# Three pieces of another size, two groups of loads put behind the token tiles, and a sum of squares spread later, in a one-core decoder layer

## The chip, the cores and the metric

The kernel runs on one core of one Trainium2 chip. Its metric is the device time of one execution in microseconds; of several executions the median counts. The core has five engines that work side by side: PE (TensorE, matrix products; its weight loads are listed as PEld), DVE (VectorE), ACT (ScalarE), POOL (GpSimd) and SP (SyncE, which here only issues DMA transfers). Each engine executes its own list of instructions in order; where an instruction needs a result of another engine or of a transfer, it waits, and all that stands behind it on that engine waits too.

## The reference

One decoder layer is applied to 1024 prompt tokens and to 64 sample tokens (8 sequences of 8) that have a cached past. All is in float32, with 1024 features.

```python
h = rmsnorm(x, lw['g_mix'])
proj = h @ lw['w_in']                       # columns: RWKV | short convolution | stick-breaking attention
o_rw, wkv_new, shift_new = rwkv7_mixer(p_rw, shift_prev, wkv_prev, lw)
o_cv, conv_new = short_conv_mixer(cb, cc, cx, conv_prev, lw['conv_w'])
o_sb = stick_breaking(q, k_all, v_all, past_len, lw['sb_bias'])
x = x + concatenate([o_rw, o_cv, o_sb]) @ lw['w_out']
h2 = rmsnorm(x, lw['g_mlp'])
x = x + square(relu(h2 @ lw['w_up'])) @ lw['w_down']
gate = sigmoid(rmsnorm(x, lw['g_ple']) @ lw['w_ple_gate'])
x = x + gate * (p @ lw['w_ple_proj'])
```

Here `rmsnorm(x, g)` is `x * rsqrt(mean(x * x) + 1e-6) * g`. In `rwkv7_mixer` each of 4 heads carries a 64x64 state through the tokens. Outputs are x, the new keys and values, and the new states.

## The kernel before

A float32 product is made of three: operand and weight are each split into a rounded high part and the rest (`wh` and `wl`, `h_hi` and `h_lo`, by a cast on ACT and a subtraction on POOL or DVE), and `wh*hi`, `wh*lo` and `wl*hi` are added up in one of eight banks of PSUM (b0 to b7), 512 columns each. Features lie on the partitions, tokens along the free axis. All 1088 tokens are worked on at once up to the mixers' outputs; from the output projection on they are two groups, A (tokens 0 to 511) and B (512 to 1087, in two pieces of 288 columns).

The stages, in the time of the profile:

- **Front, 0 to 39 us.** Nine tiles of 128 tokens (the ninth: the 64 samples) are loaded (L110), squared and summed on ACT (L189, L190), scaled on DVE (L193), transposed on PE (L198), and cast and split (L200 on ACT, L201 on DVE). SP's list holds further loads: the first weights of `w_in` (L156), 11 short loads of parameter rows into `prow` (L213, transposed at L218), 5 of small weights (L300 to L302) and the shift state `sh` (L308). The buffer `xt` has four copies: the load of tile 4 can start once tile 0 has been read.
- **RWKV projections, to 174 us.** `rw_tile` works through the tokens in the three pieces of `CH`; each is 24 products (L169 to L171) into one of banks 0 to 2. The pieces of `CH` are also used by the low-rank products, the norm of the keys, the bonus (L446 on PE, with the matrix `bones`; L447 on DVE) and the convolution.
- **Query, key and value projections, 150 to 240 us.** Groups of products (L795 to L797) fill banks 0 and 1 in turn. A bank is read by ACT twice (L802 copy `nat`, L805 square `sq`); DVE sums and scales (L807, L809, L810); PE transposes `nat` (L844). In the same stretch DVE works the function `wkv_base` (L277 to L288): a load `base_Z` of triangular 32x32 blocks, written to memory just before as `l_s` (L265), then 31 pairs of a product and a sum (L284, L286), each needing the one before, and the store `t_s` (L288). The WKV recurrence starts after it, at 217 us.
- **WKV, attention, convolution, to about 850 us; output projection, MLP and the recombined MLP of group B, to about 1580 us.** `out_proj(B)` (L1397 to L1406) lies at 1068 to 1123 us: for each of 16 groups PE makes 24 products into a bank, which DVE adds to x.
- **Last stage, from 1580 us.** The gate of group A is worked in eight steps m, while group B is prepared: the operands `op` of its norm `g_ple` (L1383 to L1392, DVE, ACT and POOL), the sum of squares (`rms`, L1327 to L1330: squares on ACT, six additions shared by POOL and DVE, one last one on DVE), its spread over the partitions (`onesq` products L1338, root L1340, reciprocal L1341, L1347, L1349), and the inputs `pn` (L1583, L1586). Block sums `s` of B's gate weights (L1430 to L1433, DVE) belong to the part that follows.

The code names work, waits and buffers; the order on each engine is not that of the code. When the program is built, a planner simulates all engines with estimated durations and takes, on each engine, what can start next. `tc.issue_after(i)` forbids it to place the instructions of the block ahead of `i`. So a change in one place can move instructions in another.

Of the kernel before, what the change touches and what calls it, by code (L numbers as in the profile page):

```python
# [33 lines left out]
NJ = 8  # L34
NS = NB * NJ
T = NP + NS
CH = ((0, 384), (384, 384), (768, 320))
C0 = math.exp(-0.5)
RMS_EPS = 1e-6
GN_EPS = 64e-5  # L40
# [8 lines left out]
def hybrid_step(ctx: ExitStack, tc: tile.TileContext, I, O):  # L49
    nc = tc.nc  # L50
    V, S, G, PE, SP = nc.vector, nc.scalar, nc.gpsimd, nc.tensor, nc.sync
# [46 lines left out]
    xp_in = I["x_prompt"][0]  # L98
    xs_in = I["x_sample"].rearrange("b j d -> (b j) d")
# [7 lines left out]
    def x_tile(i):  # L107
        r = 128 if i < 8 else NS
        xt = xpool.tile([128, D], F32, name="xt", bufs=4)
        SP.dma_start(xt[:r], xp_in[i * 128:i * 128 + 128, :] if i < 8 else xs_in)  # L110
        return xt, r

    xts = [x_tile(0)]
    gbc = xpool.tile([128, D], F32, name="gbc")
    gm = I["g_mix"]
# [65 lines left out]
    for i in range(9):  # L181
# [4 lines left out]
        xt, r = xts[i]  # L186
# [23 lines left out]
    at = 0  # L210
    for name, n in rows:
        src = I[name]
        SP.dma_start(prow[at:at + n, :], bass.AP(tensor=src.tensor, offset=src.offset, ap=[[128, n], [1, 128]]))  # L213
        col[name] = at
        at += n
    par = consts.tile([128, nrows], F32)
# [76 lines left out]
    def pe_tile(name, dtype=F32):  # L293
# [2 lines left out]

    wl2, wl2h, wl2l = (pe_tile(f"wl2{i}", d)[:, :768].rearrange("p (i c) -> p i c", i=3) for i, d in
                       enumerate((F32, F32R, F32R)))
    for s in range(2):
        SP.dma_start(wl2[64 * s:64 * s + 64, 0], I["w2"][0])  # L300
        SP.dma_start(wl2[64 * s:64 * s + 64, 1], I["a2"][0])
    SP.dma_start(wl2[:, 2], I["g2"][0])  # L302
    S.copy(wl2h, wl2)
    G.tensor_sub(wl2l, wl2, f(wl2h))
    shT = rp.tile([128, 8, NB], F32, name="shT")
# [958 lines left out]
    class Part:  # L1264
# [56 lines left out]

        def rms(self, bank, wide=False):

            sums, sq = self.act("sums", F32), [self.act("sq", F32) for _ in range(2)]
            for m in range(8):
                t = sums[:, m] if m < 2 else sq[m // 2 % 2][:, m % 2]
                S.square(t, self.x[:, m])  # L1327
                if m >= 2:
                    (G, V)[m % 2].tensor_add(sums[:, m % 2], sums[:, m % 2], t)  # L1329
            V.tensor_add(sums[:, 0], sums[:, 0], sums[:, 1])  # L1330
            self.rb = self.pool.tile([128, self.n], F32, name="rb", bufs=1)
            if not wide:

                n, ni = self.n, len(self.tiles)
                ps = bank()
                for i in range(ni):
                    e = min(n, 128 * i + 128)
                    PE.matmul(ps[:, i:i + 1], sums[:, 0, e - 128:e], onesq[:, 0:1], start=True, stop=True)  # L1338
                rs = self.pool.tile([128, ni], F32, name="rs", bufs=2)
                S.activation(rs, ps[:, :ni], AF.Sqrt, bias=eps_rms, scale=1.0 / D)  # L1340
                V.reciprocal(rs, rs)  # L1341
                for t0 in range(0, n, 512):
                    r = min(512, n - t0)
                    ps = bank()
                    for i in range(t0 // 128, -(-(t0 + r) // 128)):
                        c = min(128, n - 128 * i)
                        PE.matmul(ps[:, 128 * i - t0:128 * i - t0 + c], rs[:, i:i + 1].to_broadcast([128, 128]),  # L1347
                                  ident[:, 128 - c:], start=True, stop=True)
                    S.copy(self.rb[:, t0:t0 + r], ps[:, :r])  # L1349
            else:  # L1350
# [46 lines left out]
    def out_proj(p, k0=0, nk=8, bank=acc, order=None):  # L1397
        nm = 16 // nk
        x = [h[k0 // 4:] for h in p.h]
        for m0 in order or range(0, 8, nm):  # L1400
            w = load(w_out[k0 * 128:(k0 + nk) * 128, m0 * 128:(m0 + nm) * 128], nk, nm * 128)
            for m in range(m0, m0 + nm):
                for t0, n in p.chunks:
                    ps = bank()
                    gemm_p(ps, w, m - m0, x, t0, n, nk=nk)
                    V.tensor_add(p.x[:, m, t0:t0 + n], ps[:, :n], p.x[:, m, t0:t0 + n])  # L1406
# [140 lines left out]
        u, before = up(A, fb), u  # L1547
        down(*before)
    late = banks(0, 1, 2, 3, 4, 5)
    out_proj(B, bank=late, order=(0, 4, 2, 6))  # L1550
    u, before = up(A, NA - 1, late), u
    down(*before, bank=late)
    B.rms(banks(6, 7))
# [139 lines left out]
    for m, end in enumerate(itertools.chain.from_iterable(gate(A, sl) for sl in range(4))):  # L1693
        with tc.issue_after(end.ins):
            if m < 3:
                B.operands("g_ple", (2, 3, 1, 4), mpb, 4, ks=((0, 1), (2,), (3,))[m], out=ops)
            if m == 2:
                B.rms(banks(3, 4))
            if m == 3:
                ple_inputs(B, banks(5, 7))  # L1700
        if m == 6:
            w = {}
            pieces = gate7_weights(0, w)
            for _ in range(5):
                next(pieces)
# [38 lines left out]
```

## Time and profile before

| | |
|---|---|
| median of 3 runs | 1706.24 us (1706.22 to 1711.11) |
| the profiled execution | 1715.32 us, of which the span is 1713.5 us |
| granted TensorE clock, mean | 0.985 |
| PE busy | 1641.7 us (96% of the span) |
| PEld, DVE, ACT, POOL busy | 86%, 65%, 48%, 42% |

The profile is one execution, taken by the hardware profiler. "Busy" is time in which an instruction of the engine was under way. A row of waits reads: engine and line that waited, the engine and line it was released by, the sum, the number of times and the longest, in us. A row of the timeline reads: start in us from the span's start, duration in us, engine, line, operation, output<-inputs with partitions x elements, count; in brackets the idle time of the engine ahead of it and what ended it. Rows of PE may overlap, since products are pipelined: the distance from one start to the next is what a product costs in a dense row. `PEclk` in a table of windows is the granted share of the TensorE clock.

### The profile page before, as it was taken

The numbers are of one execution on the slowest core, as the hardware profiler recorded it, in microseconds if no ns is written. First come the engines' busy times: TensorE is split into PE (matmuls) and PEld (weight loads), VectorE is DVE, ScalarE is ACT, GpSimd is POOL, SyncE is SP. The second block draws the span as 40 slices with busy tenths as digits, with TensorE's granted clock in tenths as the row PEclk, the third lists the DMA queues.
The fourth block names the chain that finished last, engine by engine and source line by source line (L and its number), as shares of the span: only waits on it lengthen the run. The fifth ranks groups of instructions, "written<-read, shape, count | busy, mean of one in ns | idle before, by whom it ended". The sixth has DMA issues, their size and how long they took to land. (4 is left out here: it accounts for less than half of the span.)

```text
span 1713.5 us, 30844 instructions
## 1 busy us (share of the span) xinstructions
PE 1641.7 (96%) x11853; PEld 1479.4 (86%) x11853; DVE 1106.7 (65%) x1918; ACT 821.3 (48%) x1627; POOL 726.1 (42%) x778
## 2 busy tenths in 40 slices
PE   6999999999999898999999999999999999999998
PEld 5899988889888777888886777987999999999788
DVE  6266844555267759888854335277777777765896
ACT  6633433344344657666643344473443334437653
POOL 4123121123132565443334564366655455538631
PEclk9999999999999999999999999999999999999999
DMA  5134466335523764444235565322332322323332
GB/s 189 51 117 126 142 166 166 72 83 137 169 62 102 219 182 125 117 131 124 77 107 173 159 179 173 127 86 83 90 94 81 98 87 87 100 74 105 88 118 55
DMA packets 212373, 202.27 MB, mean 118 GB/s; under 512 B 58305, under 2 KB 177761, under 8 KB 212098
## 3 DMA queue, kind: packets, MB, share of 16 engines
q1 hardware_dynamic: 202498, 179.33, 35.4%
q0 software_dynamic: 5120, 16.78, 3.4%
q10 hardware_dynamic: 4608, 4.20, 1.0%
q8 instruction: 93, 1.52, 0.4%
q14 instruction: 54, 0.44, 0.1%
HBM read 163.27 MB, written 36.98 MB: 117 GB/s over the span
## 5 line engine op out<-in xcount | busy, mean ns | idle before, releaser
L1075 POOL TENSOR_TENSOR wl<-wr,wh 128x512 fp32r<-128x512 f32 x182 | 256.1, 1418 | 261.8 <-ACT wh L1074 208.5
L1074 ACT CAST wh<-wr 128x512 fp32r<-128x512 f32 x308 | 187.9, 621 | 310.9 <-PE b L1095 211.3
L1515 DVE TENSOR_TENSOR x<-b,x 128x288 f32<-128x288 f32 (+1 forms) x384 | 199.5, 529 | 96.4 <-PE b L1096 95.1
L1094 PE MATMUL b<-ah,wh 128*128 128x288 f32 (+1 forms) x768 | 253.8, 331 | 3.2 <-DVE x L1515 2.2
L1096 PE MATMUL b<-ah,wl 128*128 128x288 f32 (+1 forms) x768 | 252.6, 329 | 0.0
L1095 PE MATMUL b<-al,wh 128*128 128x288 f32 (+1 forms) x768 | 252.4, 329 | 0.0
L1094 PEld LDWEIGHTS b<-ah,wh 128*128 128x128 f32 x768 | 144.5, 188 | 15.4 <-DVE x L1515 4.6
L1096 PEld LDWEIGHTS b<-ah,wl 128*128 128x128 f32 x768 | 144.7, 188 | 10.2
L1095 PEld LDWEIGHTS b<-al,wh 128*128 128x128 f32 x768 | 144.8, 189 | 9.3 <-DVE al L1419 0.3
L795 PE MATMUL b<-wh,h_hi 128*128 128x256 f32 x432 | 128.2, 297 | 5.4 <-ACT sq L805 5.4
L1094 PE MATMUL b<-nh,wh 128*128 128x512 f32 x320 | 128.2, 401 | 2.8 <-DVE x L1406 1.6
L797 PE MATMUL b<-wh,h_lo 128*128 128x256 f32 x432 | 127.6, 295 | 0.0
L1095 PE MATMUL b<-nl,wh 128*128 128x512 f32 x320 | 127.4, 398 | 0.0
L1096 PE MATMUL b<-nh,wl 128*128 128x512 f32 x320 | 127.3, 398 | 0.0
L796 PE MATMUL b<-wl,h_hi 128*128 128x256 f32 x432 | 125.4, 290 | 0.0
L1075 DVE TENSOR_TENSOR wl<-wr,wh 128x512 fp32r<-128x512 f32 x126 | 105.2, 837 | 27.3 <-ACT wh L1074 24.4
L159 POOL TENSOR_TENSOR wl<-wr,wh 128x1024 fp32r<-128x1024 f32 x26 | 64.5, 2495 | 126.3 <-ACT wh L158 126.3
L169 PE MATMUL b<-h_hi,wh 128*128 128x384 f32 (+1 forms) x336 | 115.3, 343 | 1.9 <-ACT xs L333 1.3
L170 PE MATMUL b<-h_lo,wh 128*128 128x384 f32 (+1 forms) x336 | 114.2, 340 | 0.3 <-DVE h_lo L201 0.3
L171 PE MATMUL b<-h_hi,wl 128*128 128x384 f32 (+1 forms) x336 | 112.9, 336 | 0.0
L922 DVE TENSOR_TENSOR_SCAN keep<-keep,onesq 128x128 f32<-128x128 f32 (+3 forms) x64 | 95.6, 1494 | 21.4 <-POOL keep L920 20.7
L1446 PE MATMUL b<-op,wh 128*128 128x288 f32 x320 | 95.0, 297 | 3.1 <-DVE c L1596 1.8
(437 smaller groups left out, 4451.7 us busy)
## 6 DMA issues: line engine op xcount, KB each, us to landing
wr<-in_w_up SPq DMA_DIRECT2D x64, 512.0 KB
wr<-in_w_down SPq DMA_DIRECT2D x64, 512.0 KB
wr<-in_w_in SPq DMA_DIRECT2D x26, 512.0 KB
wr<-in_w_out SPq DMA_DIRECT2D x16, 512.0 KB
wr<-in_w_ple_gate SPq DMA_DIRECT2D x16, 512.0 KB
xt<-in_x_prompt SPq DMA_DIRECT2D x8, 512.0 KB
stk_s<-sth ACTq DMA_DIRECT2D x32, 128.0 KB
stk_s<-stl SPq DMA_DIRECT2D x32, 128.0 KB
```

Of the source, the lines that this page charges most:

```text
L169: PE.matmul(ps[:, :n], wh[:, k, c], a, start=(k == 0), stop=False)
L170: PE.matmul(ps[:, :n], wh[:, k, c], b, start=False, stop=False)
L171: PE.matmul(ps[:, :n], wl[:, k, c], a, start=False, stop=(k == nk - 1))
L795: PE.matmul(o, a, w[0][:, k, :], start=(k == 0), stop=False)
L796: PE.matmul(o, a, w[1][:, k, :], start=False, stop=False)
L797: last = PE.matmul(o, b, w[0][:, k, :], start=False, stop=(k == 7))
L1074: S.copy(h3, src)
L1075: (sub or G).tensor_sub(l3, src, f(h3))
L1094: PE.matmul(ps[:, :n], w(0, k, m), a, start=(k == 0), stop=False)
L1095: PE.matmul(ps[:, :n], w(0, k, m), b, start=False, stop=False)
L1096: PE.matmul(ps[:, :n], w(1, k, m), a, start=False, stop=(k == nk - 1))
L1515: V.tensor_add(p.x[:, m, t0:t0 + n], ps[:, :n], p.x[:, m, t0:t0 + n])
```

## The change

Four edits:

1. `CH` becomes pieces of 256, 384 and 448 tokens instead of 384, 384 and 320.
2. The 11 loads of `prow` may be placed only behind the load of x tile 5, the 5 loads of small weights only behind that of x tile 8.
3. `rms` is cut in two: `squares` (squares and their sums) and `spread` (everything from `onesq` on). For group B in the last stage, `squares` stays at step m == 2, `spread` and the inputs `pn` come at step m == 4 (before: m == 2 and m == 3).
4. `out_proj(B)` takes its banks from the default set 0, 1, 2 instead of `late`, which is 0 to 5.

```diff
-CH = ((0, 384), (384, 384), (768, 320))
+CH = ((0, 256), (256, 384), (640, 448))
...
-        SP.dma_start(xt[:r], xp_in[i * 128:i * 128 + 128, :] if i < 8 else xs_in)
+        x_dma.append(SP.dma_start(xt[:r], xp_in[i * 128:i * 128 + 128, :] if i < 8 else xs_in))
...
-        SP.dma_start(prow[at:at + n, :], bass.AP(tensor=src.tensor, offset=src.offset, ap=[[128, n], [1, 128]]))
+        with tc.issue_after(x_dma[5].ins):
+            SP.dma_start(prow[at:at + n, :], bass.AP(tensor=src.tensor, offset=src.offset, ap=[[128, n], [1, 128]]))
...
-    for s in range(2):
-        SP.dma_start(wl2[64 * s:64 * s + 64, 0], I["w2"][0])
-        SP.dma_start(wl2[64 * s:64 * s + 64, 1], I["a2"][0])
-    SP.dma_start(wl2[:, 2], I["g2"][0])
+    with tc.issue_after(x_dma[8].ins):
+        for s in range(2):
+            SP.dma_start(wl2[64 * s:64 * s + 64, 0], I["w2"][0])
+            SP.dma_start(wl2[64 * s:64 * s + 64, 1], I["a2"][0])
+        SP.dma_start(wl2[:, 2], I["g2"][0])
...
         def rms(self, bank, wide=False):
 
+            self.spread(self.squares(), bank, wide)
+
+        def squares(self):
+
             sums, sq = self.act("sums", F32), [self.act("sq", F32) for _ in range(2)]
...
             V.tensor_add(sums[:, 0], sums[:, 0], sums[:, 1])
+            return sums
+
+        def spread(self, sums, bank, wide=False):
             self.rb = self.pool.tile([128, self.n], F32, name="rb", bufs=1)
...
-    out_proj(B, bank=late, order=(0, 4, 2, 6))
+    out_proj(B, order=(0, 4, 2, 6))
...
             if m == 2:
-                B.rms(banks(3, 4))
-            if m == 3:
+                sums = B.squares()
+            if m == 4:
+                B.spread(sums, banks(3, 4))
                 ple_inputs(B, banks(5, 7))
```

Three places show what the planner makes of it; lines of the changed kernel are numbered 1 to 11 higher. The first is the start of SP's list, from the load of x tiles 1 to 3 on. Before:

```order
L110 DMA xt<-in_x_prompt 128x1024 x3
L156 DMA wr<-in_w_in 128x4x256 x2
L213 DMA prow<-in_mu_shift 8x128
L213 DMA prow<-in_w 2x128
L213 DMA prow<-in_a 2x128
L213 DMA prow<-in_k_k 2x128
L213 DMA prow<-in_k_a 2x128
L110 DMA xt<-in_x_prompt 128x1024
L213 DMA prow<-in_r_k 2x128
```

In the change:

```order
L110 DMA xt<-in_x_prompt 128x1024 x3
L157 DMA wr<-in_w_in 128x4x256 x2
L110 DMA xt<-in_x_prompt 128x1024 x2
L215 DMA prow<-in_mu_shift 8x128
L215 DMA prow<-in_w 2x128
L215 DMA prow<-in_a 2x128
L215 DMA prow<-in_k_k 2x128
L215 DMA prow<-in_k_a 2x128
L110 DMA xt<-in_x_prompt 128x1024
```

Tiles 4 and 5 stand ahead of all parameter rows. Tiles 6 and 7 are followed by four and two of them, and the small weights stand behind the samples' tile.

The second place is DVE's list at the start of `wkv_base` (lines 284 and 286 before; 286 and 288 now), beside the bonus (`xs<-b,xs`, line 447 before, 450 now) of the second half of the RWKV heads. Before:

```order
L440 SCALAR_TENSOR_TENSOR xs<-xs,par 128x1088
L284 TENSOR_TENSOR base_Q<-base_Z,base_X 128x31
L286 TENSOR_TENSOR base_X<-base_X,base_Q 128x31
L284 TENSOR_TENSOR base_Q<-base_Z,base_X 128x60
L286 TENSOR_TENSOR base_X<-base_X,base_Q 128x30x2
L447 TENSOR_TENSOR xs<-b_1607,xs 128x384
L284 TENSOR_TENSOR base_Q<-base_Z,base_X 128x87
L447 TENSOR_TENSOR xs<-b_1610,xs 128x384
L286 TENSOR_TENSOR base_X<-base_X,base_Q 128x29x3
L447 TENSOR_TENSOR xs<-b_1613,xs 128x320
```

In the change:

```order
L443 SCALAR_TENSOR_TENSOR xs<-xs,par 128x1088
L450 TENSOR_TENSOR xs<-b_1607,xs 128x256
L450 TENSOR_TENSOR xs<-b_1610,xs 128x384
L450 TENSOR_TENSOR xs<-b_1613,xs 128x448
L286 TENSOR_TENSOR base_Q<-base_Z,base_X 128x31
L288 TENSOR_TENSOR base_X<-base_X,base_Q 128x31
L286 TENSOR_TENSOR base_Q<-base_Z,base_X 128x60
```

The three additions of the bonus stood behind the first product with `base_Z`; now they stand ahead of it. On SP's list the load of `base_Z` stood ahead of `bk_s<-pinv` and of the next two halves of `w_in`; now it stands behind all three.

The third place is DVE's list at the sums of group B in the last stage (`sums`, lines 1329 and 1330 before; 1336 and 1337 now; `s` are the block sums of its gate weights). Before:

```order
L1596 TENSOR_TENSOR g<-b_18371,rb 128x512
L1329 TENSOR_TENSOR sums<-sums,sq 128x576
L1392 TENSOR_TENSOR op_18153<-tk,op_18153 128x288
L1329 TENSOR_TENSOR sums<-sums,sq 128x576 x2
L1330 TENSOR_TENSOR sums<-sums 128x576
L1430 TENSOR_TENSOR s<-wr 128x512
L1432 TENSOR_TENSOR s<-wr 128x512
```

In the change:

```order
L1336 TENSOR_TENSOR sums<-sums,sq 128x576
L1440 TENSOR_TENSOR s<-wr 128x512
L1442 TENSOR_TENSOR s<-wr 128x512
L1336 TENSOR_TENSOR sums<-sums,sq 128x576
L1608 TENSOR_TENSOR g<-b_18378,g 128x512
L1441 TENSOR_TENSOR s<-s,wr 128x512
L1336 TENSOR_TENSOR sums<-sums,sq 128x576
L1609 TENSOR_TENSOR x<-x,g 128x512
L1606 TENSOR_TENSOR g<-b_18423,rb 128x512
L1443 TENSOR_TENSOR s<-wr,s 128x512
L1337 TENSOR_TENSOR sums<-sums 128x576
```

Four block sums and three steps of group A's gate now stand among the sums, the first two block sums behind the first addition. PE's list at the `onesq` products (line 1338 before, 1348 now) has moved with it; before, they stood ahead of the last product of bank tile b_18524:

```order
L1094 MATMUL b_18524<-nh_17989,wh 128x512
L1095 MATMUL b_18524<-nl_17991,wh 128x512
L1338 MATMUL b_18353<-onesq,sums 128x1 x5
L1096 MATMUL b_18524<-nh_17989,wl 128x512
L1094 MATMUL b_18595<-nh_17988,wh 128x512
```

In the change:

```order
L1097 MATMUL b_18596<-nh_17988,wh 128x512
L1098 MATMUL b_18596<-nl_17990,wh 128x512
L1348 MATMUL b_18469<-onesq,sums 128x1 x5
L1099 MATMUL b_18596<-nh_17988,wl 128x512
L1618 MATMUL b_18561<-ident,x 128x128 x4
```

They now come after one more product of b_18524, 12 of b_18595 and 11 of b_18596, the last step's two tiles, and after 12 products of the gate's second factor (`ph`, `pl`) that before came behind them.

More of the change, by code (lines that the diff above doesn't have):

```diff
@@ L109, in x_tile @@
         xt = xpool.tile([128, D], F32, name="xt", bufs=4)
-        SP.dma_start(xt[:r], xp_in[i * 128:i * 128 + 128, :] if i < 8 else xs_in)
+        x_dma.append(SP.dma_start(xt[:r], xp_in[i * 128:i * 128 + 128, :] if i < 8 else xs_in))
         return xt, r
+    x_dma = []
     xts = [x_tile(0)]
```

## The prediction

> **What bounds the kernel now.** I read the page's head first, then the waits of PE over the whole run, then a table of windows for the stages that the edits touch.
>
> ```profile
> PE 1641.7 (96%) x11853; PEld 1479.4 (86%) x11853; DVE 1106.7 (65%) x1918; ACT 821.3 (48%) x1627; POOL 726.1 (42%) x778
> ```
>
> ```profile
> PE b L198 <- POOL mfull L237: 8.0, 1, 8.0
> PE b L795 <- ACT sq L805: 5.4, 1, 5.4
> PE b L198 <- DVE h L193: 3.8, 3, 2.2
> PE b L1338 <- DVE sums L1330: 3.4, 1, 3.4
> PE b L512 <- DMA bk<-bk_s: 2.2, 2, 2.0
> ```
>
> PE is busy for 1641.7 of 1713.5 us, so 72 us is all that any re-ordering can win, plus time in which PE runs slowly. The first wait is the arrival of the first tile, which no edit touches. The third is in the front. The second and the fourth lie at the two places where the planner's lists move.
>
> ```profile
> 160.00:185.00 25.00, 19.62 (x136) 18.72 (x135) 17.61 (x46) 5.94 (x11) 0.00 (x0) 0.86 0.59 147
> 217.00:225.00 8.00, 5.84 (x36) 4.88 (x36) 1.05 (x3) 2.49 (x5) 1.26 (x1) 0.79 0.60 136
> 1597.00:1645.00 48.00, 43.10 (x208) 35.71 (x206) 38.71 (x51) 29.07 (x59) 24.44 (x17) 0.93 0.40 123
> 1068.00:1123.00 55.00, 55.00 (x421) 54.49 (x420) 18.39 (x32) 24.11 (x42) 19.18 (x16) 1.00 0.43 138
> ```
>
> The columns are the window, its length, then PE, PEld, DVE, ACT and POOL busy, the granted clock, the DMA share and GB/s. PE is full in `out_proj(B)` (1068 to 1123). In the other three it is not, and there the clock is below 1 too.
>
> **Pieces and banks: 0.** What a product costs is its distance to the next in a dense row:
>
> ```profile
> 23.81 0.33 PE L170 MATMUL b<-h_lo,wh 128*128 128x384 f32 x1
> 23.98 0.33 PE L171 MATMUL b<-h_hi,wl 128*128 128x384 f32 x1
> ...
> 180.23 0.28 PE L797 MATMUL b<-wh,h_lo 128*128 128x256 f32 x1
> 180.35 0.28 PE L795 MATMUL b<-wh,h_hi 128*128 128x256 f32 x1
> ```
>
> 384 columns cost 0.17 us, 256 cost 0.12. On the line through them 320 costs 0.147 and 448 costs 0.20. Three pieces: before 0.174 + 0.174 + 0.147 = 0.495, now 0.12 + 0.174 + 0.20 = 0.494. Numbers of products are unchanged, so this edit is worth nothing in the dense part. With fewer banks, `out_proj(B)` needs a bank back after two further groups of 24 products, at least 2 x 24 x 0.12 = 5.8 us, while one addition on DVE takes about half a microsecond (the same shape as at L1515 in the row below). It is covered tenfold; without the cover each of 16 groups would pay 0.5 us. I take 0 for both, ends -0.5 and +0.8.
>
> ```profile
> L1515 DVE TENSOR_TENSOR x<-b,x 128x288 f32<-128x288 f32 (+1 forms) x384 | 199.5, 529 | 96.4 <-PE b L1096 95.1
> ```
>
> **The front: 0.** Tile 4's load stood behind five short ones:
>
> ```profile
> 6.54 1.28 DVE L193 SCALAR_TENSOR_TENSOR h<-xt,rs,gbc 128x1024 f32<-128x1024 f32 x1 [0.38 <-DMA gbc<-in_g_mix]
> 10.42 0.36 SPq L110 DMA_DIRECT2D xt<-in_x_prompt  x1
> 19.14 0.36 SPq L110 DMA_DIRECT2D xt<-in_x_prompt  x1
> 25.20 2.34 PE L198 MATMUL b<-ident,h 128*128 128x128 f32 x20
> 26.65 1.05 ACT L158 CAST wh<-wr 128x1024 fp32r<-128x1024 f32 x1 [2.93 <-DMA wr<-in_w_in]
> 29.34 0.66 PE L198 MATMUL b<-ident,h 128*128 128x128 f32 x4 [1.80 <-DVE h_lo L201]
> ```
>
> Its buffer is free when tile 0 is scaled (6.54 + 1.28 = 7.8), so it can start 2.6 us earlier than 10.42. Tile 7, the last of its kind, was issued at 19.14 and keeps nine parameter rows ahead of it; I take 17.5. PE did not wait for tile 4 itself: it was in the first piece until 25.2, then waited at 29.34 for evictions behind ACT's cast at 26.65, which waits for weights. That cast is still ahead of tile 4's casts on ACT. A first piece of 256 ends earlier, yet it leaves 128 columns x 24 products = 24 x 0.053 = 1.3 us for the third. The gain is bounded by tile 4's 2.6 us, the loss by one more slow stretch like that of the next part, 2.3 us. Both ends are near; I take 0, since the last tile moves least.
>
> **At the query and key products: -2.5.** Here DVE, not ACT, is what PE waits for:
>
> ```profile
> 165.32 1.87 SPq L277 DMA_DIRECT2D base_Z<-l_s  x2
> 171.37 0.19 DVE L284 TENSOR_TENSOR base_Q<-base_Z,base_X 128x31 f32<-128x31 f32 x1 [6.70 <-DMA base_Z<-l_s]
> 173.48 0.48 DVE L447 TENSOR_TENSOR xs<-b,xs 128x320 f32<-128x320 f32 x1
> 174.05 0.60 ACT L805 ACTIVATE sq<-b 128x512 f32<-128x512 f32 x1 [11.69 <-DMA wr<-in_w_in]
> 174.70 0.58 PE L795 MATMUL b<-wh,h_hi 128*128 128x256 f32 x1 [5.38 <-ACT sq L805]
> 175.50 0.41 PE L795 MATMUL b<-wh,h_hi 128*128 128x256 f32 x1
> 175.72 0.41 PE L796 MATMUL b<-wl,h_hi 128*128 128x256 f32 x1
> 180.48 0.68 DVE L810 TENSOR_TENSOR nat<-nat,ss 128x512 f32<-128x512 f32 x1
> ```
>
> DVE stood 6.70 us at L284 for `base_Z`; the bonus additions L447 stood behind it. The square L805, whose buffer is taken over from the bonus's inputs, starts right after the last of them (173.96), and PE, which needs the bank that L805 reads, 0.65 us later. The release named for L805 is a weight load that its data does not need. The idle is 5.38 us; then some 25 products cost 0.21 instead of 0.12 us, 25 x 0.09 = 2.3 us. Together 7.7 us.
>
> In the change the additions stand ahead of L284. Their products on PE end at about 167, three additions of half a microsecond bring 168.7, the square another 0.6: PE stops for some 0.6 us instead of 5.4. What is late next: 48 products of 0.12 us on (5.8 us, to about 175.8), PE transposes `nat`, which needs L810; L810 is still behind `base_Z`, and about 5.3 us of DVE and ACT work lies between the landing and its end (171.37 to 181.16 in the rows, less what DVE did for other parts). `base_Z` itself now stands behind `bk_s` (0.54 MB) and two halves of weights (1.05 MB). At 147 GB/s for a share of 0.59, so 249 GB/s for a full one, that is 0 to 6.3 us later. I take 2, because one of the halves is issued ahead of all blocks and the store of `xs` too is issued earlier. Then `nat` is ready at 173.4 + 5.3 = 178.7, a stall of 2.9 us, and I add 1.7 us for a slow stretch: in the window from 217 a wait of 2.0 us for `bk` went with a clock of 0.79, 8 x 0.21 = 1.7 us lost. The rest is 0.6 + 2.9 + 1.7 = 5.2, the gain 2.5 us. Ends: landing unmoved, 0.6 + 0.9 left, gain 6.2; landing 6.3 later, 0.6 + 7.2 + 1.7 left, loss 1.8.
>
> The Trainium skill, "TensorE: Matmul & The Clock Gate", Part 1, says that the clock falls to half after about 3.4 us without work. By it a stall of 2.9 us would cost no slow stretch, and this term would be -4.2. The window from 217 speaks against it: there 2.0 us was enough, so I keep the 1.7.
>
> **The last stage: -5.** The sums of group B end late; beside POOL's work an addition takes 1.86 us, alone 0.77:
>
> ```profile
> 1606.07 0.68 DVE L1596 TENSOR_TENSOR g<-b,rb 128x512 f32<-128x512 f32 x1
> 1606.67 0.77 DVE L1329 TENSOR_TENSOR sums<-sums,sq 128x576 f32<-128x576 f32 x1
> 1607.36 1.68 DVE L1392 TENSOR_TENSOR op<-tk,op 128x288 fp32r<-128x288 f32 x1
> 1608.96 3.72 DVE L1329 TENSOR_TENSOR sums<-sums,sq 128x576 f32<-128x576 f32 x2
> 1612.78 1.63 DVE L1330 TENSOR_TENSOR sums<-sums 128x576 f32<-128x576 f32 x1
> 1613.83 0.37 SPq L1068 DMA_DIRECT2D wr<-in_w_ple_gate  x1
> 1617.61 0.69 DVE L1430 TENSOR_TENSOR s<-wr 128x512 f32<-128x512 f32 x1 [3.19 <-DMA wr<-in_w_ple_gate]
> 1610.69 0.40 PE L1095 MATMUL b<-nl,wh 128*128 128x512 f32 x1
> 1614.47 2.29 PE L1338 MATMUL b<-onesq,sums 128*128 128x1 f32 x10 [3.38 <-DVE sums L1330]
> 1618.05 0.63 PE L1096 MATMUL b<-nh,wl 128*128 128x512 f32 x1
> 1618.47 0.63 PE L1094 MATMUL b<-nh,wh 128*128 128x512 f32 x1
> ```
>
> PE loses 3.4 us of idle, then nine products cost 0.43 instead of 0.23 us (1.8 us), and of the 2.29 us of `onesq` perhaps 1 is the slow clock: 6.2 us. In the change 24 gate products and 12 of the second factor more lie ahead of `onesq`: 36 x 0.228 = 8.2 us, so PE comes at 1611.1 + 8.2 = 1619.3. DVE has more ahead of it as well. Counted in the durations of these rows from 1606.07: one g, two op, four sums, four s and four steps of the gate, 0.68 + 3.36 + 6.1 + 2.8 + 2.7 = 15.6, to 1621.7; if sums run beside no POOL work (0.77 each, as the first one), to about 1618.8. In the middle lies 1620.3, a stall of 1 us. The block sums wait for weights that landed at 1617.6; their load is released by POOL's splits (`wl`), which before alternated with POOL's share of the sums and now stand ahead of it, and I take them as landed. The gain is 6.2 - 1.0 = 5 us. DVE can carry it: it was idle for 48.0 - 38.7 = 9.3 us in that window. Ends: 7 gained, or, with the landing unmoved, the case of the loss below.
>
> **The sum.** 0 + 0 - 2.5 - 5 = -7.5. The profiled execution took 1715.32 us, its span 1713.5 and 1.8 around it; changed, 1707.8. The median of the runs shown is 9.1 us below that execution, so the prediction is 1698.7, said as 1699.
>
> **The rivals.** The measurement can tell about 0.3% (5.1 us) from no change.
>
> - *The waits only move.* One of the two places gives nothing: `nat` stalls on a late `base_Z` for all that the square no longer waits, or the sums on DVE end as late against PE as before. For it: in both lists the same landing or the same additions still stand ahead of PE's next need. Against: PE has 5.8 and 8.2 us of other work there. -5 or -2.5: 1701 to 1704.
> - *The front shortens too.* Three tile loads come 1.6 to 2.6 us earlier; if the last tiles set the start of the dense part, another 2.6: 1696. Against it stands the cast at 26.65.
> - *The change does not do what it says.* Neither place nor the front gains: 1706. Only the coverage above speaks against it.
> - *Slower: the sums wait for a load.* The first two block sums now stand between the sums. If their weights land at 1617.6 as before, the rest (0.69 x 4 + 1.86 x 2 + 1.63 + 2.1, 10.2 us) ends at 1627.8; PE, there at 1619.3, stands 8.5 us and then runs 1.8 + 1 slowly: 11.3 against 6.2, a loss of 5, which with nothing gained at the query and key products gives 1711. It costs more than the old wait once the landing is later than 1619.3 + 3.4 - 10.2 = 1612.5. For it: the load was issued at 1613.83, 3.8 us ahead of its landing, so it must be issued 5 us earlier; against it: POOL's splits, which release it, have moved ahead.
>
> **How the numbers follow.** Forecast 0.42 (its own range 1694 to 1701), waits move 0.27, front too 0.14, no effect 0.07, slower 0.10. The second case ends at 1701 at best, just at the bound; I give 0.02 of it to faster. So faster is 0.42 + 0.14 + 0.02 = 0.58, same 0.25 + 0.07 = 0.32, slower 0.10. The range from 1692 to 1707 leaves out the slow case and the far end of the front's.
>
> **What would show it.** Right: PE's wait at L798 (now) for the square is under 1 us; a wait at L847 for `nat` takes its place, 1 to 4 us; PE's wait at L1348 is under 2 us and the clock from 1610 to 1630 near 1. The dense part after the front starts within 2 us of 39. Wrong: a wait over 5 us at L847, a wait at L1336 or L1440 for a `wr` load while PE stands at L1348, or a new wait in `out_proj(B)`.

## The result and the profile after

The change made the kernel slower: 1725.5 us median against 1706.2, ratio 1.0108 with a 95% interval of 1.0087 to 1.0128. Forecast were 1699 us and a range of 1692 to 1707.

The head of the page after, the row of busy times:

```profile
PE 1648.2 (95%) x11853; PEld 1475.2 (85%) x11853; DVE 1116.5 (65%) x1918; ACT 820.5 (48%) x1627; POOL 726.9 (42%) x778
```

The waits of PE over the whole run after, in the columns of the prediction:

```profile
PE b L199 <- POOL mfull L239: 8.1, 1, 8.1
PE b L199 <- DVE h L194: 4.6, 4, 1.8
PE b L847 <- DVE nat L813: 4.5, 1, 4.5
PE b L956 <- DVE wtl L61: 4.3, 4, 1.4
PE b L945 <- DVE beta L927: 4.1, 2, 3.8
PE b L1307 <- DMA xr<-in_x_prompt: 3.9, 4, 2.6
PE b L580 <- DVE Wm L573: 3.1, 1, 3.1
PE b L945 <- DVE wtl L61: 3.0, 1, 3.0
```

The waits for `sq` and for `sums` are gone, as forecast. What stands in their place is not one wait but many groups of 2 to 4.5 us in sum, most of them on DVE. Apart from the one for `nat`, which the prediction foretold, the new ones lie in stages of which it doesn't speak. The windows show where. First those of before (window, length, then PE, PEld, DVE, ACT, POOL busy, granted clock, DMA share, GB/s), in the WKV stage, in attention beside the first output product of group A, and in the last stage:

```profile
340.00:385.00 45.00, 45.00 (x616) 39.27 (x616) 23.38 (x54) 17.18 (x39) 11.20 (x10) 1.00 0.30 82
560.00:600.00 40.00, 33.80 (x218) 28.18 (x217) 29.36 (x82) 26.36 (x60) 23.32 (x39) 0.96 0.76 233
600.00:685.00 85.00, 75.99 (x350) 60.81 (x350) 63.25 (x70) 55.27 (x103) 51.25 (x57) 0.98 0.53 154
```

The same windows after, and the last stage in the window that the prediction quoted:

```profile
340.00:385.00 45.00, 41.88 (x572) 36.27 (x571) 24.58 (x50) 14.80 (x35) 10.19 (x8) 0.92 0.29 82
560.00:600.00 40.00, 31.89 (x224) 26.46 (x222) 29.73 (x76) 23.77 (x53) 21.75 (x37) 0.91 0.69 211
600.00:685.00 85.00, 70.85 (x309) 54.72 (x310) 55.61 (x61) 47.95 (x89) 47.05 (x52) 0.96 0.49 141
...
1597.00:1645.00 48.00, 42.13 (x194) 34.14 (x193) 42.74 (x53) 32.50 (x63) 29.77 (x22) 0.96 0.28 83
```

In the WKV window PE had been full at full clock; now it idles 3 us and the clock is 0.92. From 560 to 685 us it idles 22.3 us where it had idled 15.2.

The most useful view is one worked out from the two traces: the start of the n-th PE instruction in a kernel's profiled run, less its start in the run before. The marks are times in the run before. All kernels of the later sections are in it, so that it can be looked up:

```
mark (us)          50   200   250   325   400   440   560   640   700  1000  1580  1700
the change       -5.2  -4.5  -3.2  -4.6  +1.2  -0.0  +2.5 +12.9 +16.1 +13.9 +15.1 +13.9
e1 pieces        -0.4  +1.1  +2.4  +0.5  +5.1  +3.8  +8.4 +19.9 +19.3 +17.4 +18.3 +17.4
e2 loads         -3.2  -3.5  -2.8  -5.2  -3.7  -4.4  -3.5  +3.8  +9.4  +7.2  +8.2  +6.0
e3 spread        +0.0  -0.8  -0.9  -5.2  -5.2  -5.2  -7.0  -6.0  -7.3 -10.7  -9.9 -15.9
e4 banks         -1.9  -3.1  -3.0  -7.1  -7.1  -7.1  -9.1  -4.9  -7.8  -9.6  -9.0  -6.9
h1 loads held    -0.2  -1.8  -3.0  -7.4  -7.4  -7.3  -6.8  -2.5  -5.3  -6.8  -5.9  -8.2
h2 pieces held   -1.7  -0.9  +4.0  +0.1  +0.1  -1.2  -1.0  -0.7  -0.7  -2.3  -1.6  -2.9
h3 three held    -2.3  -1.3  +2.1  -2.1  -2.1  -3.4  -2.2  -0.2  -1.6  -4.9  -3.9  -6.9
h4 two held      -3.9  -4.4  -4.5  -9.2  -9.2  -9.2  -8.5  -6.5  -9.3 -10.6 -10.0 -16.3
k1 other lists   +0.3  -0.4  -2.7  -4.5  -3.0  -3.7  -3.8  +2.5  +8.1  +5.2  +5.6  +4.8
k2 held late     -1.5  -2.1  -3.7  -5.0  -3.5  -4.2  -5.3  -2.6  -5.1  -7.7  -7.5  -8.3
k3 held mid      -3.3  -2.6  -1.4  -2.8  +3.2  +1.9  +3.4  +5.1  +3.9  +0.5  +0.5  -0.7
k4 rows, spread  -3.4  -3.7  -4.0  -8.3  -8.3  -8.3 -10.1  -9.2  -9.2 -11.8 -11.8 -18.2
s1 one row moved +1.0  +0.6  +1.0  -1.5  -0.1  -0.7  -1.8  +0.2  +6.3  +1.7  +1.4  +1.6
s2 held early    -3.3  -2.6  +0.9  -3.6  -3.6  -4.8  -3.2  +1.4  -1.4  -6.0  -7.0  -6.8
s3 before, e1's  +1.5  +1.4  +0.4  -0.3  +4.2  +4.2  +4.1 +15.2 +14.8  +8.4  +8.6  +6.2
```

The run before lies 9 us above its median and loses some 4 us to a slow stretch at 279 us that none of the other runs in the table has; so read the steps along a row, and compare rows with each other, not with zero. Steps of 2 to 3 us can be such stretches too, since they differ from run to run. The changed kernel gains 5 us in the front, keeps them to 325 us, loses 6 by 400, and loses 16 more between 440 and 700. The last stage, where the prediction saw the greatest gain, brings 1.2.

### The profile page after: what moved, and what is told of

It reads as the page before. It is cut to its first block, busy times and chain, and to the rows that moved or that the text cites. A ratio compares the mean times of both kernels' runs of the same rounds, so it can differ in the third digit from the quotient of the medians.

```text
span 1727.3 us, 30841 instructions
## 1 busy us (share of the span) xinstructions
PE 1648.2 (95%) x11853; PEld 1475.2 (85%) x11853; DVE 1116.5 (65%) x1918; ACT 820.5 (48%) x1627; POOL 726.9 (42%) x778
## 4 chain that ended last, share of the span: by engine, by line
PE 71%; DVE 12%; DMA 8%; issue 3%; ACT 3%; SPq 2%; POOL 1%; ACTq 0%; DVEq 0%; POOLq 0%
PE b L1097 11%; PE b L1099 11%; PE b L1098 11%; PE b L1458 3%; PE b L1456 3%; PE b L1457 3%; PE b L171 3%; PE b L170 3%; PE b L172 3%; PE b L800 2%; PE b L798 2%; PE b L799 2%; PE b L945 1%; DMA wr<-in_w_up 1%; DMA wr<-in_w_out 1%
## 5 line engine op out<-in xcount | busy, mean ns | idle before, releaser
L1078 DVE TENSOR_TENSOR wl<-wr,wh 128x512 fp32r<-128x512 f32 x126 | 101.1, 805 | 28.7 <-ACT wh L1077 26.2
L170 PE MATMUL b<-h_hi,wh 128*128 128x256 f32 (+2 forms) x336 | 114.7, 342 | 3.1 <-ACT h_hi L201 1.4
L171 PE MATMUL b<-h_lo,wh 128*128 128x256 f32 (+2 forms) x336 | 114.2, 340 | 0.1
L172 PE MATMUL b<-h_hi,wl 128*128 128x256 f32 (+2 forms) x336 | 114.1, 340 | 0.0
```

What stands on the lines that cost most here:

```text
L170: PE.matmul(ps[:, :n], wh[:, k, c], a, start=(k == 0), stop=False)
L171: PE.matmul(ps[:, :n], wh[:, k, c], b, start=False, stop=False)
L172: PE.matmul(ps[:, :n], wl[:, k, c], a, start=False, stop=(k == nk - 1))
L1078: (sub or G).tensor_sub(l3, src, f(h3))
```

## Which of the four edits loses the time

The edits one by one, each on the kernel before. Two theories stood against each other: the pieces lose it (P), or the loads (L).

**e1, the pieces alone.**

```diff
-CH = ((0, 384), (384, 384), (768, 320))
+CH = ((0, 256), (256, 384), (640, 448))
```

> Only the pieces are changed (256, 384, 448 tokens). Against the profile of before, the changed kernel was 5 us ahead at 50 us, lost 6 us at 350 us (inside the WKV recurrence) and 12 us between 575 and 665 us, and gained nothing in the last stage. Theory P, the pieces: other pieces give the planner other durations, and its new lists for WKV and attention hold the waits; this kernel then is 10 to 20 us slower than before (1716 to 1726). Theory L, the loads: the moved loads shift the planner's clock, and its lists from the query products on; this kernel is then within 5 us of before, and about 2 us slower in the front, where 128 columns wait for the third piece.

**e2, both groups of loads alone.**

```diff
+        with tc.issue_after(x_dma[5].ins):
             SP.dma_start(prow[at:at + n, :], ...)
...
+    with tc.issue_after(x_dma[8].ins):
         for s in range(2):
             SP.dma_start(wl2[64 * s:64 * s + 64, 0], I["w2"][0])
```

> Only the 11 parameter loads and the 5 small weights are put behind the x tiles; the pieces stay 384, 384, 320. Theory P: a gain of 2 to 5 us in the front and no loss behind it, 1701 to 1706. Theory L: the gain of the front, and then the waits at 350 us and from 575 to 665 us as in the changed kernel, 1715 to 1725.

**e3, the sums and their spread alone.**

```diff
             if m == 2:
-                B.rms(banks(3, 4))
-            if m == 3:
+                sums = B.squares()
+            if m == 4:
+                B.spread(sums, banks(3, 4))
```

> Only the spread of group B's sums and its inputs come at step 4. Its lists differ from those of before only in the last stage. My prediction had -5 us for it (1701). Theories P and L both say that the last stage lost nothing by itself: between -5 and +1 us (1701 to 1707). The profile of the changed kernel (PE waits of 2.3 us at the onesq products and 2.7 us at a transpose of the output) makes 0 the nearest.

**e4, three banks alone.**

```diff
-    out_proj(B, bank=late, order=(0, 4, 2, 6))
+    out_proj(B, order=(0, 4, 2, 6))
```

> Only the output projection of group B uses three banks instead of six. All theories: 0, at most 1 us (1705 to 1708); 24 products lie between two uses of a bank.

Measured, against 1708.3 us for the kernel before:

| | median us | ratio, 95% interval |
|---|---|---|
| e1 pieces | 1729.4 | 1.0126 (1.0091 to 1.0161) |
| e2 loads | 1722.8 | 1.0097 (1.0067 to 1.0128) |
| e3 spread | 1701.9 | 0.9969 (0.9953 to 0.9986) |
| e4 banks | 1710.7 | 1.0029 (1.0012 to 1.0045) |

Neither theory holds: each of the two early edits, alone, loses about as much as all four together. Losses that don't add up are a sign that both set off the same thing. In the table both lose at the same place, from 560 to 700 us (e1 from 340 on as well), most of it far behind the instructions that they touch: the loads are in the front, and of the pieces only the convolution's products come later, from 440 to 570 us. What both have in common is that the planner, once something differs ahead of 200 us, draws other lists for the stages up to 764 us (e1) and 805 us (e2); behind that, PE's list is again that of before, row for row, to the end. The sums, which change nothing ahead of the last stage, gain what was forecast. The banks, which were to cost nothing, cost 0.3%.

## The same edits with the old lists

The theory that follows (D): the drawn lists cost the time, not the edits. It can be tested by keeping an edit and handing the planner the order of another kernel. A function of 25 lines at the end of the program does it: on each engine each instruction may be placed only behind its predecessor in a stored list. No wait is added or taken away.

```diff
     with tile.TileContext(nc, schedule_with_timeline_sim=True) as tc:
         hybrid_step(tc, ins, outs)
+        hold(tc, nc)
...
+    for engine in (ET.PE, ET.DVE, ET.Activation, ET.Pool, ET.SP):
+        own = [i for i in traced if i.engine == engine]
...
+        for a, b in zip(chain, chain[1:]):
+            tc.add_manual_dep(b, a.name, dep, reason="issue_after")
```

The lists are held from the 1241st PE instruction on; in the trace that is at some 215 us, behind the front and the first query products (the first expectation puts it at 100 us, which was an error). Ahead of it each kernel has its own lists.

**h1, the loads with the lists of before.**

> The two load edits alone, as in the run that was 0.97% slower than before, but from the 1241st PE instruction on (the last stretch of the front, some 100 us into the span) all five engines get the lists of the kernel before, word for word. Nothing of the work differs. Theory D (drawn lists: an edit ahead of 150 us makes the planner draw other lists for everything up to 680 us, and before's happen to run better on the chip): the loss is gone and the front's 3 to 5 us stay, 1700 to 1705 us, ratio 0.995 to 0.999. Theory E (the edit itself costs, by late parameters, colliding transfers or an unlucky meeting with the clock): the loss stays, 1715 to 1725 us, ratio 1.005 to 1.010.

**h2, the pieces with the lists of before.**

> The pieces alone, as in the run that was 1.3% slower, again with the lists of the kernel before from the 1241st PE instruction on; the shapes of the piece-wise products and transposes differ, their number and sequence don't. Theory D: 1703 to 1710 us, ratio 0.998 to 1.002, as the work is the same and the front moved by under 1 us. Theory E: 1718 to 1732 us, ratio 1.007 to 1.014. In between (1711 to 1717): the pieces cost something of their own, in the convolution's products or at the end of the front, and the lists the rest.

**h3, pieces, loads and spread with the lists of e3.**

> Pieces, loads and spread sums (all of the change but the three banks), with the lists of the kernel that had only the spread sums (0.31% faster than before) from the 1241st PE instruction on. Theory D: the front's 3 to 5 us and the last stage's 5 to 6 us both stay, 1695 to 1701 us, ratio 0.993 to 0.997. Theory E: the pieces and the loads bring their 14 to 21 us along, 1712 to 1725 us, ratio 1.003 to 1.010.

**h4, loads and spread with the lists of e3.**

> Loads and spread sums, pieces of before, with the same lists of the kernel that had only the spread sums. Theory D: 1695 to 1701 us, ratio 0.993 to 0.997, within 2 us of the run with the new pieces; where it lies below that one by more, the pieces cost the difference by themselves. Theory E: 1708 to 1718 us, ratio 1.001 to 1.006.

| | own lists | held lists |
|---|---|---|
| loads | 1.0097 (e2) | 0.9967 (0.9952 to 0.9981), 1703.6 us |
| pieces | 1.0126 (e1) | 1.0017 (1.0003 to 1.0031), 1711.4 us |
| pieces, loads, spread | not run | 0.9984 (0.9972 to 0.9997), 1706.4 us |
| loads, spread | not run | 0.9935 (0.9918 to 0.9952), 1697.9 us |

The loads turn from a loss of 1.0% to a gain of 0.3%, and the pieces' loss shrinks from 1.3% to 0.2%, with not one instruction of the work different. h1 and h4 lie in their bands, h2 at the upper edge of its own (the ratio inside, the time 1.4 us above), h3 above its own: the pieces have a cost of their own, 0.2% by h2 and 0.5% by h3 against h4. Its greatest piece is at the start of the WKV stage. The waits of PE from 130 to 260 us in h3, which has the new pieces:

```profile
PE b L515 <- DMA bk<-bk_s: 5.9, 1, 5.9
PE b L847 <- DVE nat L813: 4.4, 1, 4.4
```

And in h4, which has the old ones and otherwise the same lists:

```profile
PE b L798 <- ACT sq L808: 5.6, 1, 5.6
PE b L515 <- DMA bk<-bk_s: 1.9, 1, 1.9
PE b L847 <- ACT nat L849: 0.7, 1, 0.7
```

The wait for `bk` grows from 1.9 to 5.9 us, 4 of the 8.5 us that lie between the two. Why `bk` lands later was not tried.

**k1, the reverse: the kernel before, with the lists of e2.** If the lists alone carry the loss, the untouched kernel must lose it too.

> The kernel before, not one load moved and the pieces of before, but from the 1241st PE instruction on (some 215 us into the span) with the lists that the planner drew for the kernel with the two load edits. Theory D (the lists cost, not the edits): as much slower as that kernel was behind its front, 1717 to 1727 us, ratio 1.006 to 1.012. Theory E (the loads cost by themselves, and the lists held in the runs before hid it in some other way): 1704 to 1711 us, ratio 0.998 to 1.002.

1720.4 us, ratio 1.0072 (1.0050 to 1.0095).

**s3, the kernel before with the lists of e1.**

> The kernel before, pieces of before, with the lists that the planner drew for the kernel with the new pieces, from the 1241st PE instruction on. A second drawn list on work that hasn't changed. If drawn lists as such run worse here than the one of before: 1717 to 1728 us, ratio 1.006 to 1.012. If only the lists of the load edits were bad, and the pieces cost by themselves: 1705 to 1712 us.

1721.2 us, ratio 1.0098 (1.0066 to 1.0130). Two different drawn lists on unchanged work both cost 0.7 to 1.0%. Theory D holds, in both directions.

**k2, the loads with the lists of before from the 3001st PE instruction on, some 440 us.**

> The two load edits; the planner's own lists up to the 3001st PE instruction (some 440 us), from there on those of the kernel before. If the loss of the load edits stands in the stage from 560 to 680 us (attention beside the first group's output product), where the profile of that kernel fell back by 8 us against before, nearly all of it goes: 1702 to 1707 us. If it stands in the lists of the WKV stage ahead of 440 us, 1714 to 1722 us. If half and half, 1708 to 1713 us.

1707.2 us, ratio 0.9986 (0.9971 to 1.0000): of the 1.3% between e2 and h1, 1.1 stand behind 440 us.

**k3 and s2, the whole change with the lists of before from 440 to 720 us, and from 215 to 720 us.** Everything else is drawn by the planner, the last stage and the banks too.

> The whole change, with the planner's own lists everywhere but between the 3001st and the 4450th PE instruction (some 440 to 720 us), where the five engines get the lists of the kernel before. The changed kernel fell back by 8 to 10 us in that stretch and by some 10 us at 340 to 380 us. Theory D: the first of the two goes, 1714 to 1719 us, ratio 1.003 to 1.007. If the stretch only hands on a lateness from ahead of it: 1722 to 1730 us.

> The whole change with the lists of the kernel before from the 1241st to the 4450th PE instruction (some 215 to 720 us), where the run before held only 440 to 720 us and came to 1714 us. What is added is the WKV stage, in which the changed kernel fell back by 10 us at 340 to 380 us; against it stands the wait for bk at 215 us, which the pieces brought with held lists (6 us for 2). If the WKV list costs what its profile showed: 1706 to 1710 us. If the wait at 215 us eats it: 1712 to 1716 us.

k3: 1714.1 us, ratio 1.0041 (1.0028 to 1.0053). s2: 1708.5 us, ratio 1.0012 (0.9994 to 1.0029). So of the change's 1.08%, 0.67 stand between 440 and 720 us and another 0.29 between 215 and 440 (each a difference of two ratios, each known to 0.1 or 0.2). In s2 the wait at L515 is back at 6.0 us, and the WKV stage gains more than it takes.

## What is wrong with a drawn list

Between 340 and 380 us the changed kernel loses 6 us at one place. Its timeline:

```profile
348.80 4.88 POOL L160 TENSOR_TENSOR wl<-wr,wh 128x1024 fp32r<-128x1024 f32 x2 [9.22 <-ACT wh L159]
...
349.32 2.15 DVE L611 TENSOR_TENSOR yc<-yc,sqy 128x256 f32<-128x256 f32 x1
...
351.51 2.51 DVE L613 TENSOR_SCALAR yc<-yc,par 128x128 f32<-128x128 f32 x2
...
355.02 0.41 DVE L573 COPY Wm<-b 128x256 f32<-128x256 f32 x1
...
355.49 1.12 PE L580 MATMUL b<-AB,Wm 64*64 64x128 f32 x8 [3.12 <-DVE Wm L573]
```

Before, the same DVE operations, three numbers lower by line:

```profile
352.31 0.42 DVE L608 TENSOR_TENSOR yc<-yc,sqy 128x256 f32<-128x256 f32 x1
...
353.24 0.59 DVE L610 TENSOR_SCALAR yc<-yc,par 128x128 f32<-128x128 f32 x2
...
353.75 0.96 DVE L570 COPY Wm<-b 128x256 f32<-128x256 f32 x2
...
359.23 4.70 POOL L159 TENSOR_TENSOR wl<-wr,wh 128x1024 fp32r<-128x1024 f32 x2 [3.77 <-ACT wh L158]
```

A DVE operation that takes 0.42 us took 2.15, and a pair that takes 0.59 took 2.51 (its first half 2.25), beside POOL's two splits of a weight (`wl`, 2.4 us apiece); each was held until about the end of one split. Before, the splits ran some 7 us later against these operations, behind the chain that PE waits for. In the changed kernel PE stood 3.1 us for it, and what follows shows the second half of the price (the window behind the wait, after):

```profile
355.50:362.00 6.50, 6.50 (x48) 5.71 (x49) 2.19 (x5) 0.00 (x0) 1.53 (x2) 0.51 0.56 141
```

PE is busy throughout, at a clock of 0.51: another 3 us. The same pair, a stretched DVE operation and a half-clock stretch, stands in k1 at 586 us, where attention's small steps pass between PE, ACT and DVE while the first output product is to fill PE:

```profile
586.51 4.54 DVE L1292 TENSOR_TENSOR ml<-mixl,mh 128x512 fp32r<-128x512 f32 x1 [0.53 <-ACT mh L1291]
586.79 3.70 POOL L1075 TENSOR_TENSOR wl<-wr,wh 128x512 fp32r<-128x512 f32 x3
...
590.98 0.41 DVE L956 TENSOR_TENSOR o<-b,o 64x256 f32<-64x256 f32 x1
...
585.80 0.47 PE L1094 MATMUL b<-mh,wh 128*128 128x512 f32 x1
586.12 0.40 PE L1095 MATMUL b<-ml,wh 128*128 128x512 f32 x1
591.44 0.58 PE L952 MATMUL b<-wth,vs 128*128 128x256 f32 x1 [4.92 <-DVE o L956]
```

In the kernel before:

```profile
590.31 0.42 DVE L956 TENSOR_TENSOR o<-b,o 64x256 f32<-64x256 f32 x1 [0.27 <-ACT o L955]
...
590.06 0.48 PE L1094 MATMUL b<-mh,wh 128*128 128x512 f32 x1
...
592.89 0.39 PE L1095 MATMUL b<-ml,wh 128*128 128x512 f32 x1
593.12 0.28 PE L952 MATMUL b<-wth,vs 128*128 128x256 f32 x1
```

The list of before puts 13 products of the output projection ahead of PE's next attention step (3 us of cover) and no wide DVE operation ahead of `o`. The drawn list puts 2 products (0.6 us) there, and DVE's `ml` ahead of `o`. How long `ml` takes in the kernel before (least, median and longest of 16, in ns):

```profile
L1292 DVE TENSOR_TENSOR ml<-mixl,mh x16: 672/748/1711, 575.3 to 1075.7; 128x512 fp32r<-128x512 f32 x8, 128x576 fp32r<-128x576 f32 x8
```

It takes 4.54 us in the drawn list.

**s1, k1 with a single row moved.** On DVE `ml` goes behind `o` and one `wtl`; all other rows of all engines stay.

```diff
 L61 TENSOR_TENSOR wtl<-b_6762,wth 128x256
-L1292 TENSOR_TENSOR ml_6895<-mixl,mh_6893 128x512
 L956 TENSOR_TENSOR o_6757<-b_6729,o_6757 64x256
 L61 TENSOR_TENSOR wtl<-b_6762,wth 128x128
+L1292 TENSOR_TENSOR ml_6895<-mixl,mh_6893 128x512
```

> The kernel before with the other lists (1720 us, ratio 1.0072), and one row of them moved: on VectorE the low part of a 512-wide operand (L1292 ml), which took 4.54 us beside POOL's three subtractions (L1075) where its median is 0.74, goes behind the two small operations that stood after it (L956 o and L61 wtl). PE stood 4.9 us for that o at 586.5 us and then ran 6.8 us at half clock. Theory F (these waits, behind VectorE operations stretched by POOL, and the half clock after them are what a drawn list costs): PE's wait there falls below 1 us and the half clock after it goes, 1711 to 1716 us, ratio 1.002 to 1.005. If what follows has to wait for the moved operation in its turn, or PE's gain is given back at the next meeting: 1718 to 1723 us.

The timeline of s1 at the place:

```profile
587.96 3.76 POOL L1075 TENSOR_TENSOR wl<-wr,wh 128x512 fp32r<-128x512 f32 x3
588.04 0.42 DVE L956 TENSOR_TENSOR o<-b,o 64x256 f32<-64x256 f32 x1 [0.50 <-ACT o L955]
...
588.51 0.39 PE L952 MATMUL b<-wth,vs 128*128 128x256 f32 x1 [0.44 <-DVE o L956]
588.58 3.70 DVE L1292 TENSOR_TENSOR ml<-mixl,mh 128x512 fp32r<-128x512 f32 x1
```

`ml` is stretched as before (3.70 us beside POOL), but nobody waits for it now: PE's wait falls from 4.92 to 0.44 us. The window behind it, first in k1, then in s1:

```profile
592.00:600.00 8.00, 8.00 (x33) 6.51 (x32) 2.71 (x6) 2.98 (x7) 2.23 (x2) 0.77 0.48 149
```

```profile
589.00:597.00 8.00, 7.78 (x39) 6.46 (x38) 6.35 (x8) 2.82 (x7) 5.28 (x5) 1.00 0.56 178
```

From 580 to 600 us s1 wins 5.8 us on k1. Of that 3 to 4 are left at the end: 1716.4 us, ratio 1.0057 (1.0040 to 1.0075), between the two bands that were expected, with an interval that overlaps k1's. So the mechanism is shown at this place; that one row carries a fifth to a third of k1's loss of 12 us is what the profile, the medians and the ratios say between them, and the times alone don't prove it. The other waits of the drawn lists were read from traces and not undone one by one, and whether the planner's estimates lack the stretching was not tried. The sums do fit: between the marks 560 and 700 the changed kernel takes 13.6 us longer than the one before, PE idles 8.2 us more, and 6.9 us more at half clock cost another 3.4.

**k4, the best version.** With the parameter rows moved, but not the small weights, PE's list is that of e3 to the last row, so nothing has to be held.

```diff
+        with tc.issue_after(x_dma[5].ins):
             SP.dma_start(prow[at:at + n, :], ...)
...
-                B.rms(banks(3, 4))
-            if m == 3:
+                sums = B.squares()
+            if m == 4:
+                B.spread(sums, banks(3, 4))
```

> Only the parameter rows moved behind the sixth x tile, and the sums spread later; small weights, pieces and banks of before, and no list held. The planner draws PE's list for it as for the kernel with the spread sums alone, to the last row, so no list is drawn anew ahead of the last stage. By theory D it keeps the front's gain (if that is the rows': PE's first products waited for the transfers of the x tiles) and the last stage's: 1695 to 1700 us, ratio 0.992 to 0.996. If the front's gain was the small weights', 1700 to 1704 us.

1696.7 us, ratio 0.9933 (0.9911 to 0.9956). It beats both kernels: against the whole change 29 us. With the rows alone moved the lists stay, with the small weights moved too (e2) they are drawn anew, so it is the small weights that set the planner off. How much the rows gain by themselves is less sure. The profile of k4 is 3.4 us ahead at 50 us, but 1.7 of that is clock: the run before has 3.4 us at half clock from 40 us on, and k4, like e4, which is 1.9 us ahead with no edit in the front, has none. From 30 to 50 us, the kernel before, then k4:

```profile
30.00:50.00 20.00, 18.37 (x107) 17.27 (x108) 9.69 (x21) 8.84 (x23) 2.41 (x6) 0.91 0.10 27
...
30.00:50.00 20.00, 19.29 (x125) 18.36 (x125) 9.19 (x22) 10.33 (x22) 2.26 (x5) 1.00 0.08 24
```

Some 1.5 us in the front, k4's lead on e4, are the rows' own.

## Why the prediction was wrong

**The step that failed** is a sentence ahead of the sum: "The second and the fourth lie at the two places where the planner's lists move." The lists had moved from the front to 805 us, and the sum has no term for it. The profile was read for waits that the edits touch, and all other stages were carried over at their old price. None of the rivals is this mechanism; "slower", at 0.10, named another one, at a load that PE did not come to wait for. The forecast missed by 26.5 us; 17 of them are what s2 gives back by holding 215 to 720 us. The prediction's signs of being wrong had the same blind spot: none of the three came (PE stood 4.5 us at L847, not over 5; no DVE operation stood for a weight load while PE stood at L1348; `out_proj(B)` lost 0.2 us), and the kernel was slower all the same. By its own terms:

- *Pieces and banks, 0.* Right for the products, nearly: the rows of 0.12 and 0.17 us stayed as they were, and the 336 of 448 columns cost 0.206 us, not 0.20, which makes some 2 us. Wrong for the rest. The pieces cost 0.2 to 0.5% with held lists, mainly by the wait for `bk`. The banks cost 0.3% (e4), not in `out_proj(B)`, where PE was busy 54.77 of 55 us after, but in the last stage, where the list was drawn anew: there e4's profile has a wait that the one before has not.

```profile
PE b L1347 <- DVE rs L1341: 4.3, 1, 4.3
```

- *The front, 0.* Off in the profile of the change, which is 5.2 us earlier at 50 us, beyond the end of -2.6. But 1.7 of the 5.2 are the half clock at 40 us that the run before had and this one not; with the old pieces and the same loads moved the runs are 0.2 (h1, with 6.8 us at half clock) to 3.9 us earlier (h4, with none). With half of the time at half clock taken off, all four runs of that front (e2, h1, h4, k2) reach the mark after 46.1 to 46.8 us, the six without any edit there (before, e3, e4, k1, s1, s3) after 47.6 to 48.6: by this estimate the moved loads bring 1.5 to 2 us, inside the stated ends. The rest of the 5.2 came with the pieces, of which the first is narrower; with the pieces alone, h2 is 1.7 us ahead at 50 us and 0.9 at 200. By the times, k4 against e3, 1696.7 against 1701.9 us with the same PE list, the rows would be worth 5 us, but the two intervals touch, so the 5 is not firm.
- *At the query and key products, -2.5.* The chain after:

```profile
163.87 0.62 DVE L450 TENSOR_TENSOR xs<-b,xs 128x448 f32<-128x448 f32 x1 [0.20 <-PE b L449]
164.58 0.60 ACT L808 ACTIVATE sq<-b 128x512 f32<-128x512 f32 x1 [5.67 <-DVE xs L450]
...
171.52 0.19 DVE L286 TENSOR_TENSOR base_Q<-base_Z,base_X 128x31 f32<-128x31 f32 x1 [7.03 <-DMA base_Z<-l_s]
...
175.43 0.68 DVE L813 TENSOR_TENSOR nat<-nat,ss 128x512 f32<-128x512 f32 x1
176.17 1.11 PE L847 MATMUL b<-ident,nat 128*128 128x128 f32 x4 [4.54 <-DVE nat L813]
```

  The square is free of `base_Z` and PE stands for `nat` instead, as the working said; the size that failed is the delay of `base_Z`. It was taken as 2 us and was 4: from the first store of the blocks `l_s` to the first product with `base_Z` it took 14.9 us before and 19.1 after.

```profile
156.49 6.11 SPq L265 DMA_DIRECT2D l_s<-LT  x4
...
152.44 1.29 SPq L267 DMA_DIRECT2D l_s<-LT  x2
```

  In all six profiled runs with the new pieces it took 18.8 to 19.5 us, and PE stood 4.2 to 5.0 us for `nat`, whether the front was early or late; in the eleven with the old pieces it took 13.6 to 15.2 us. In the profile of the change the landing stands at the old time (171.5 against 171.4) only because everything ahead of it came 4 us earlier, PE too: it was there at 171.6 and not at 175.8. So PE stood 4.5 instead of 2.9 us. The clock then fell as much as before (0.86 in the window from 160 to 185, both times), so the term came to nothing: -4.5 us ahead of the place, -4.5 behind it. That is the rival "the waits only move".
- *The last stage, -5.* Right where it stands alone: e3 gains 0.31%, 5.3 us, and 6 us in its profile, with no wait at the `onesq` products. In the whole change the planner drew this stage differently again, and 1.2 us are left: from the mark 1580 to the mark 1700 PE idles 6.8 us, where it idles 3.2 in e3 and 6.9 before. The banks seem to be what has it drawn anew, since of e1, e2 and e4 only e4 changes PE's list there; e3 and the banks together were not run. The waits of PE from 1590 to 1660 us after:

```profile
PE b L1618 <- ACT yt L1619: 2.6, 1, 2.6
PE b L1348 <- DVE g L1608: 2.3, 1, 2.3
```

  L1348, the `onesq` products, is where the forecast said under 2 us. The sums were not late: they ended at 1640.0 us, when PE came. It waited for `g` (L1608), which on DVE stood behind a `wl`. L1618, the output's transposes, it didn't name; e3 has a wait of 2.7 us at these too, and still gains.

## What to carry over

Where a planner orders the work, an edit has two prices: what it does at its place, and what every list drawn behind it turns into. Before the first is worked out, compare the lists of the two kernels from end to end, and where they differ on unchanged work, give that a term of its own, with room for a loss. All three lists that were drawn here for the stages up to 800 us (the change, e1, e2) ran worse than the one in hand, by 0.7 to 1.3%; for the last stage one was better (e3) and one worse (e4). Whether a loss is the rule, one kernel can't show. A held list separates the two prices in one run, and an edit that leaves the lists alone (here the parameter rows, without the small weights) keeps its gain.

## What was not expected of the hardware

Which DVE operation is stretched beside POOL's split of a weight, and which isn't. In s1, during the same 3.76 us of `wl` on POOL, `o<-b,o` took its usual 0.42 us and `ml<-mixl,mh` 3.70; the first reads a bank of PSUM and one tile, the second two tiles. One tile and a column of parameters (`yc<-yc,par`, L613) were not safe either: 2.25 us against a median of 0.34. The Trainium skill, "SBUF — State Buffer", in its summary of rules, says that a DVE operation with two SBUF inputs and a GpSimd one that reads SBUF block each other until the first is finished. The trace agrees on `o` and `ml`. In k1 `ml` began at 586.51, ahead of POOL's first `wl` at 586.79 (POOL's issue of a gather, `kpg`, was under way until 586.76), and ended at 591.05, after all three of them; in the changed kernel `yc<-yc,sqy` ended at 351.47, soon after the first of two splits.

A wait of 3.1 us on PE cost 6: the 6.5 us behind it in the changed kernel ran at a clock of 0.51. The Trainium skill, "TensorE: Matmul & The Clock Gate", Part 1, puts the fall to half after a window of about 3.4 us without work; here 3.12 us were enough, and where PE stood 2.0 us for `bk` in the kernel before, the window had a clock of 0.79.
